# HGRN2 and latent-attention trunk on one core: block decays and 1/rms steps kept in PSUM, and two re-ordered entries

## The chip, the cores and the metric

The kernel runs on one core of a Trainium2 chip. The metric is the time of one execution in microseconds (us), as the device measures it. A kernel is run several times and the median counts.

## What is computed

Two layers over 1024 tokens of width 1024, all in float32. Cut to what matters:

```python
# layer 0
h = h + hgrn2_mixer(rmsnorm(h), ...)          # 8 heads of 128
h = h + square(relu(rmsnorm(h) @ w_up0)) @ w_dn0
# shared keys and values, then layer 1
ckr = rmsnorm(h) @ w_dkv                      # 256 latent + 64 rope columns
c_kv = rmsnorm(ckr[:, :256]); k_rope = rope(ckr[:, 256:])
c_q = rmsnorm(rmsnorm(h) @ w_dq)              # 256 columns
h = h + causal_attention(c_q @ w_uq, c_kv @ w_uk, c_kv @ w_uv, k_rope) @ w_o   # 16 heads
h = h + square(relu(rmsnorm(h) @ w_up1)) @ w_dn1
return rmsnorm(h)

def hgrn2_mixer(xn):                          # per head, chunks of 64 tokens
    q = silu(xn @ w_q); f = lb + (1 - lb) * sigmoid(xn @ w_f); k = 1 - f; v = xn @ w_i
    # inside a chunk: score(t, s) = sum_d q[t,d] * k[s,d] * prod(f[s+1..t, d]), s <= t
    # across chunks: state = prod(f) * state + (k * decays)^T v
```

## The kernel before

Every large product is made of three TensorE passes over operands split in a rounded part ("h") and a rest ("l"): wh·xh, wh·xl, wl·xh (`mm3`, line 99 for the projections). A weight that arrives by DMA is rounded on ACT (`load`, L135) and its rest is made on POOL (L138, a subtraction of two SBUF tiles of 128x1024). Work is written in program order with priorities, and a scheduler sets each engine's order from that; `tc.high_priority(offset)` moves a piece up, and `tc.issue_after(mark)` holds it behind a named matmul.

PSUM has eight banks of 128x512 float32: four of a tag `x` (HGRN) or `ps` (MLP) or two pairs of a tag `s` (attention), three of tag `mm`, and one, `nb`.

**HGRN (start to about 610 us).** 16 units, one for each head and half of the sequence. `project` makes the unit's f, k, q, values and gate by L99 matmuls; `core` makes the decayed scores. The products q·k with their decays are built by doubling block lengths h = 1, 2, 4, 8, 16, 32. At each length `grow` multiplies the k of the left half blocks (L342) and the q of the right half blocks (L344) by the block decay totals `tot`, and then multiplies neighbouring totals to those of the doubled blocks (L347), in SBUF tiles. For h of 4 and more the scores of a level are eight small matmuls (L366; two for each of four chunks) into a PSUM bank, of which columns 0 to 255 are used, and `put` (L323) copies them under a mask to ST. TensorE runs the level's L366 between the projections (L99) of the next unit.

**MLP.** Two-by-two block products by a seven-multiplication scheme; in `up_first` the products B11, B21, T1, B22, T2, T3, T4 of two halves e go to banks, and the combinations C00, C01, C11, C10 are summed on VectorE (DVE) (L729, L737, L739) and scaled by the token's 1/rms with the relu (L680). The 1/rms (`inverse`, L575 to L582) is a sum over partitions by a matmul, ACT's Ln and Exp, and one Newton step (`newton`, L110 to L112) over SBUF tiles. L818 are the matmuls of the product that follows (`down`), L802 adds their sums to the residual.

**Attention entry (1300 to 1410 us).** `cproj(w, i, u)` makes 128 columns i (0, 1: keys and values; 3, 4: queries; 2: rope) of half u: 24 L99 matmuls of 128x512 into one `mm` bank. After i = 1 it issues `inv_rms` (squares L481, sums L483, a matmul L489 behind the mark, then L491 to L493 and the Newton step), and L983 scales each bank by the result and frees it. The order is i = 0, 1, 3, 4, 2 for half 0 and then half 1, with `norm_kv` and `norm_q` (the second rmsnorms, again through L489, and L502, L92) between. L1107 are the score matmuls, L1147 transposes of probabilities, `fO` the outputs times w_o (L99 again).

## Time and profile before

| | |
|---|---|
| median of 3 runs | 2790.72 us (2789.53 to 2794.49) |
| profiled execution | 2790.73 us; its span 2788.9 us, so 1.8 us lie around the span |
| mean granted TensorE clock | 0.986 |
| TensorE busy | 2642.7 us (95%) |
| DVE, ACT, POOL busy | 1870.4, 1185.5, 1393.9 us |

"Idle before" is the time an engine sat still before an instruction, and the arrow names the engine, tile and line that released it. [...]

### The profile page before, as it was taken

How to read it: one execution, taken by the hardware profiler on the slowest of the kernel's cores; microseconds unless marked ns; L12 is line 12 of the kernel's file. 1: busy time of each engine (PE TensorE's matmuls, PEld its weight loads, DVE VectorE, ACT ScalarE, POOL GpSimd, SP SyncE). 2: the span in 40 equal slices, each digit the busy share in tenths (PEclk: the TensorE clock that was granted, in tenths of full speed). 3: DMA queues.
4: the chain of work that ended last, by engine and by line, in shares of the span. 5: the costliest groups of instructions: out<-in, count | busy, mean ns of one | idle time of the engine just before them, and what ended most of it. 6: DMA issues, size and time to landing. Idle time of an engine off the chain costs nothing.

```text
span 2788.9 us, 35224 instructions
## 1 busy us (share of the span) xinstructions
PE 2642.7 (95%) x13137; PEld 2182.1 (78%) x13137; DVE 1870.4 (67%) x2986; ACT 1185.5 (43%) x2262; POOL 1393.9 (50%) x865
## 2 busy tenths in 40 slices
PE   7999999999899999998799999999999899999997
PEld 6878877787688888877578888888877688888885
DVE  5566666658676666669776666676668755565667
ACT  4222223235334343446354444444445644444445
POOL 3222223456677777776221223122315677777776
PEclk9999999999999999999899999999999999999999
DMA  4111112242111111111111111111101211111111
GB/s 134 40 34 38 31 39 61 61 117 79 45 51 53 50 46 61 61 57 34 48 44 35 29 48 37 42 29 48 44 14 39 65 53 51 56 61 61 61 47 63
DMA packets 184632, 143.99 MB, mean 52 GB/s; under 512 B 12497, under 2 KB 156046, under 8 KB 184462
## 3 DMA queue, kind: packets, MB, share of 16 engines
q1 hardware_dynamic: 184462, 141.75, 16.8%
q8 instruction: 103, 1.69, 0.3%
q14 instruction: 67, 0.55, 0.1%
HBM read 133.33 MB, written 4.19 MB: 49 GB/s over the span
## 4 chain that ended last, share of the span: by engine, by line
PE 67%; DVE 13%; POOL 6%; issue 6%; ACT 5%; DMA 2%; SPq 0%; DVEq 0%; POOLq 0%; ACTq 0%
PE mm L99 21%; PE ps L818 8%; PE ps L669 7%; PE mm L669 7%; PE mm L818 6%; PE s L1107 5%; PE nb L1140 3%; POOL wl L534 3%; PE nb L818 2%; PE mm L1147 2%; PE x L366 2%; POOL wu L534 2%; DVE fr L534 1%; DMA dn<-mlp_w_down 1%; ACT P L1113 1%
## 5 line engine op out<-in xcount | busy, mean ns | idle before, releaser
L99 PE MATMUL mm<-xn,wh 128*128 128x512 f32 x1728 | 571.3, 405 | 10.9 <-DVE res L802 5.2
L534 POOL TENSOR_TENSOR wl<-dn,wh 128x512 fp32r<-128x512 f32 x224 | 367.5, 1661 | 137.7 <-ACT wh L621 121.6
L99 PEld LDWEIGHTS mm<-xn,wh 128*128 128x128 f32 x1728 | 322.9, 191 | 75.6 <-issue 8.9
L99 PE MATMUL mm<-xn,wl 128*128 128x512 f32 x864 | 347.8, 403 | 2.0 <-POOL wl L138 2.0
L138 POOL TENSOR_TENSOR wl<-wst,wh 128x1024 fp32r<-128x1024 f32 (+1 forms) x93 | 221.2, 2382 | 256.1 <-ACT wh L135 253.6
L534 POOL TENSOR_TENSOR wl<-wu,wh 128x512 fp32r<-128x512 f32 x160 | 232.2, 1462 | 62.3 <-ACT wh L621 60.4
L621 ACT CAST wh<-wu 128x512 fp32r<-128x512 f32 x216 | 130.6, 618 | 242.1 <-POOL wu L534 123.5
L792 ACT CAST hh<-fr 128x1024 fp32r<-128x1024 f32 x112 | 118.0, 1053 | 270.6 <-PE ps L818 132.4
L1116 POOL TENSOR_SCALAR P<-P,rc 128x128 f32<-128x128 f32 (+1 forms) x64 | 52.9, 826 | 347.9 <-DVE rc L1114 303.5
L534 POOL TENSOR_TENSOR wu<-wu,wu 128x512 f32<-128x512 f32 x120 | 175.1, 1459 | 92.8 <-DVE wl L534 42.1
L534 DVE TENSOR_TENSOR hl<-fr,hh 128x1024 fp32r<-128x1024 f32 x112 | 199.9, 1793 | 21.3 <-ACT hh L792 20.9
L534 POOL TENSOR_TENSOR dn<-dn 128x1024 f32<-128x1024 f32 x64 | 178.6, 2791 | 45.2 <-DMA dn<-mlp_w_down 41.4
L99 PEld LDWEIGHTS mm<-xn,wl 128*128 128x128 f32 x864 | 165.1, 191 | 33.9 <-POOL wl L138 2.4
L534 DVE TENSOR_TENSOR fr<-fr 128x1024 f32<-128x1024 f32 x68 | 131.7, 1937 | 50.3 <-ACT fr L675 48.7
L1113 ACT ACTIVATE P<-s,mx 128x384 f32<-128x384 f32 (+7 forms) x128 | 95.2, 743 | 138.6 <-DVE mx L1111 119.9
L621 ACT CAST wh<-dn 128x512 fp32r<-128x512 f32 x224 | 129.9, 615 | 25.2 <-PE ps L669 10.7
L1140 PE MATMUL nb<-h,xn 128*128 128x256 f32 (+1 forms) x640 | 134.2, 288 | 0.2
L1062 POOL TENSOR_TENSOR P<-P,sin 128x512 f32<-128x512 f32 x16 | 21.7, 1356 | 215.9 <-DMA P<-P 215.9
L669 PE MATMUL ps<-xn,wh 128*128 128x512 f32 x512 | 127.3, 390 | 2.3 <-DVE xn L534 1.5
L91 ACT CAST h<-mm 128x512 fp32r<-128x512 f32 (+1 forms) x160 | 82.8, 547 | 104.8 <-PE mm L1147 104.8
L669 PE MATMUL mm<-xn,wh 128*128 128x512 f32 x496 | 122.8, 389 | 0.0
L92 DVE TENSOR_TENSOR l<-mm,h 128x512 fp32r<-128x512 f32 (+1 forms) x160 | 97.0, 633 | 30.2 <-ACT h L91 29.9
(400 smaller groups left out, 6937.4 us busy)
## 6 DMA issues: line engine op xcount, KB each, us to landing
dn<-mlp_w_down SPq DMA_DIRECT2D x64, 512.0 KB, 3.9
wu<-mlp_w_up SPq DMA_DIRECT2D x122, 256.0 KB, 2.9
wst<-hgrn_w_o SPq DMA_DIRECT2D x16, 512.0 KB, 3.9
wst<-mla_w_o SPq DMA_DIRECT2D x16, 512.0 KB, 3.7
wst<-hgrn_w_q SPq DMA_DIRECT2D x10, 512.0 KB, 3.8
wst<-hgrn_w_i SPq DMA_DIRECT2D x10, 512.0 KB, 3.9
wst<-hgrn_w_g SPq DMA_DIRECT2D x10, 512.0 KB, 3.8
wst<-hgrn_w_f SPq DMA_DIRECT2D x9, 512.0 KB, 3.8
```

The source lines that it names most:

```text
L91: S.copy(out=out_h, in_=src)
L92: V.tensor_tensor(out=out_l, in0=src, in1=out_h.bitcast(F32), op=ALU.subtract)
L99: m = T.matmul(ps, l, r, start=i == 0, stop=i == n - 1)
L138: G.tensor_tensor(out=wl[:, cs], in0=st[:, cs], in1=wh[:, cs].bitcast(F32), op=ALU.subtract)
L534: return eng.tensor_tensor(out=out, in0=x, in1=y, op=op)
L621: S.copy(out=wh, in_=x)
L669: m = T.matmul(bank, l[:, k, :], r[:, k, :], start=start and n == 0, stop=n == 11, skip_group_check=not start)
L792: cast = S.copy(out=hh, in_=Bq)
L818: T.matmul(banks[i], l, r, start=start and k == 0 and n == 0, stop=k == 1 and n == 2, skip_group_check=not start)
L1107: T.matmul(ps[:, at + u * HALF:at + u * HALF + w_], l, r, start=e == 0, stop=e == len(terms) - 1)
L1113: S.activation(out=pt[:, :n], in_=sc, func=AF.Exp, bias=mx, accum_out=sm)
L1140: T.matmul(dst, l, r[:, cols_], start=j == 0 and e == 0, stop=j == 2 * g + 1 and e == 2)
```

## The change

1. **Decays.** `grow` gets a room in PSUM: the totals of h = 1, 2 are written to unused columns of the bank that held the sums of h = 1, those of h = 4 to 32 to columns 256 and up of the level's own score bank. The multiplications of k and q read the totals there; ACT copies each to SBUF, for the second operand of the next product.
2. **1/rms.** The variance and the Newton steps stand in the bank that the sum was made in.
3. **First MLP's `up_first`.** C11 += T3's bank and C01 += B22's come first (the one with a raised priority), then T4 of both halves, then the relus.
4. **Attention entry.** i = 0, 1 go to a pair of banks of tag `s`; the sums of squares are listed ahead; 1/rms comes after i = 3; the second norms move later; the first key and query products are held behind marks.
5. **Last outputs.** Three outputs of half 1 of the pair before go ahead of the last pair's outputs of half 0.

```diff
-            tot = f
+            tot = f, f
-            def grow(h, tot):
+            def grow(h, tot, room=None):
                 n = 512 // (2 * h)
-                t2 = tot.rearrange("p (b two) -> p b two", two=2)
+                t2, c2 = (t.rearrange("p (b two) -> p b two", two=2) for t in tot)
...
                 nt = sb(f"tot{h}", 2, (P, n))
-                V.tensor_tensor(out=nt, in0=t2[:, :, 0], in1=t2[:, :, 1], op=ALU.mult)
-                return nt
-            tot = grow(1, tot)
+                if room is None:
+                    V.tensor_tensor(out=nt, in0=t2[:, :, 0], in1=c2[:, :, 1], op=ALU.mult)
+                    return nt, nt
+                V.tensor_tensor(out=room, in0=t2[:, :, 0], in1=c2[:, :, 1], op=ALU.mult)
+                S.copy(out=nt, in_=room)
+                return room, nt
+            low = ps
+            tot = grow(1, tot, low[:, 256:512])
...
-            tot = grow(2, tot)
+            tot = grow(2, tot, low[:, 0:128])
...
-                tot = grow(h, tot)
+                tot = grow(h, tot, ps[:, 256:256 + 256 // h] if h < 64 else None)
+            tot = tot[1]
...
     def inv_rms(tmp, src, n, mark=None, acc=None):
+        acc = squared(tmp, src, n) if acc is None else acc
...
-        V.tensor_scalar(out=v, in0=ps, scalar1=1.0 / (n * P), scalar2=EPS, op0=ALU.mult, op1=ALU.add)
-        newton(y, v, t)
-        return y
+        V.tensor_scalar(out=ps, in0=ps, scalar1=1.0 / (n * P), scalar2=EPS, op0=ALU.mult, op1=ALU.add)
+        newton(y, ps, ps, None if n == KT else ps)
+        return y if n == KT else ps
...
-                V.tensor_scalar(out=acc, in0=ps, scalar1=1.0 / D, scalar2=EPS, op0=ALU.mult, op1=ALU.add)
-                newton(y, acc, t)
+                V.tensor_scalar(out=ps, in0=ps, scalar1=1.0 / D, scalar2=EPS, op0=ALU.mult, op1=ALU.add)
+                newton(y, ps, ps)
...
                 for e in two:
+                    with tc.high_priority(offset=40):
+                        V.tensor_tensor(out=C[e][1, 1], in0=C[e][1, 1], in1=x[e], op=ALU.add)
+                    V.tensor_tensor(out=C[e][0, 1], in0=C[e][0, 1], in1=z2[e], op=ALU.add)
+                each("T4", x, w, False)
+                for e in two:
+                    relu(0, C[e][1, 0], x[e])
+                for e in two:
                     relu(0, C[e][0, 0])
-                    V.tensor_tensor(out=C[e][0, 1], in0=C[e][0, 1], in1=z2[e], op=ALU.add)
+                    relu(1, C[e][1, 1])
                     relu(1, C[e][0, 1])
-                    V.tensor_tensor(out=C[e][1, 1], in0=C[e][1, 1], in1=x[e], op=ALU.add)
-                    relu(1, C[e][1, 1])
-                    product(x[e], w[e], "T4", False, True)
-                    relu(0, C[e][1, 0], x[e])
...
-            ps = bank()
+            if i == 0:
+                pairs[u] = bank2("s", 2, 1024)
+            ps = pairs[u][:, i * 512:(i + 1) * 512] if i < 2 else bank()
...
-                cmark.append(mm3(ps, [(wh[:, k, :], wl[:, k, :], xh[:, k, :], xl[:, k, :]) for k in range(KT)]))
-                if (i, u) in ((1, 0), (1, 1)):
-                    inv[u] = inv_rms(ntmp, lambda k: hT[u][:, k, :], KT, cmark[-1])
-                    for i, ps in held.pop(u, []) + [(i, ps)]:
+                terms = [(wh, xh, k) for k in range(KT)] + [(wl, xh, k) for k in range(KT)]
+                terms = terms[:4] + terms[8:12] + [(wh, xl, k) for k in range(4)] + terms[4:8] + terms[12:] + \
+                    [(wh, xl, k) for k in range(4, KT)]
...
+                if u not in inv:
+                    held.setdefault(u, []).append((i, ps))
+                if i == 3:
+                    inv[u] = inv_rms(ntmp, lambda k: hT[u][:, k, :], KT, cmark[-1], sums[u])
+                    for i, ps in held.pop(u):
                         scaled(i, u, ps)
...
+        sums = [squared(ntmp, lambda k: hT[0][:, k, :], KT)]
         for i in (0, 1, 3, 4, 2):
             cproj(wc[i], i, 0)
+        sums.append(squared(ntmp, lambda k: hT[1][:, k, :], KT))
...
+        cproj(wc[0], 0, 1)
+        with tc.high_priority(offset=150):
+            norm_kv(0, cmark[4])
+            norm_q(0, cmark[5])
...
-                todo = [t for t in todo if t[1] == 0] + [(p, 0, d) for d in range(KT)] + [t for t in todo if t[1]]
+                rest = [t for t in todo if t[1]]
+                todo = [t for t in todo if t[1] == 0] + rest[:3] + [(p, 0, d) for d in range(KT)] + rest[3:]
```

In the changed kernel the line numbers are a little higher: `grow` is L343, L345, L351 (L352 is the ACT copy), the level's matmuls L372, the entry's projections L994, the sums' matmul L500, the MLP's L740, L749, L748 stand for L729, L737, L739, and `down` is L832.

How the order moves, at three places. First DVE in HGRN, around the levels h = 4 to 16 of one unit (k_1082 and q_1111 before, k_1094 and q_1123 now); the names with f are the next unit's h = 1. Before:

```order
L323 COPY_PREDICATED ST_205<-masks,x_1533 112x16x16
L342 TENSOR_TENSOR k_1082<-k_1082,tot_286_1531 128x16x16
L344 TENSOR_TENSOR q_1111<-q_1111,tot_286_1531 128x16x16
L270 TENSOR_TENSOR prl_1756<-pr_1753,prh_1755 128x256
L342 TENSOR_TENSOR k_1378<-k_1378,f_1376 128x256
L344 TENSOR_TENSOR q_1407<-q_1407,f_1376 128x256
L323 COPY_PREDICATED ST_205<-masks,x_1543 96x8x32
L342 TENSOR_TENSOR k_1082<-k_1082,tot_288_1541 128x8x32
L344 TENSOR_TENSOR q_1111<-q_1111,tot_288_1541 128x8x32
```

Now:

```order
L323 COPY_PREDICATED ST_205<-masks,x_1533 124x64x4
L343 TENSOR_TENSOR k_1094<-k_1094,x_1507 128x64x4
L345 TENSOR_TENSOR q_1123<-q_1123,x_1507 128x64x4
L351 TENSOR_TENSOR x_1533<-x_1507,tot_282_1530 128x64
L270 TENSOR_TENSOR prl_1780<-pr_1777,prh_1779 128x256
L345 TENSOR_TENSOR q_1425<-q_1425,f_1394 128x256
L323 COPY_PREDICATED ST_205<-masks,x_1544 120x32x8
L343 TENSOR_TENSOR k_1094<-k_1094,x_1533 128x32x8
L345 TENSOR_TENSOR q_1123<-q_1123,x_1533 128x32x8
L351 TENSOR_TENSOR x_1544<-x_1533,tot_284_1541 128x32
```

The k and q products of a level now read a PSUM bank (x_...), and the product of totals (L351) stands inside the chain of levels; the levels lie later against the next unit's h = 1.

Second DVE in `up_first` of the first MLP, from the second half's Newton step to the sums that T4 waits for (ps_5723 and mm_5724, ps_5819 and mm_5820 are the banks of T3 and T4). Before:

```order
L112 SCALAR_TENSOR_TENSOR row<-hl_5638,row 128x512
L729 TENSOR_TENSOR fr<-fr,mm_5819 128x512
L737 TENSOR_TENSOR fr<-fr,ps_5866 128x512
L680 SCALAR_TENSOR_TENSOR fr<-fr,row 128x512 x2
L739 TENSOR_TENSOR fr<-fr,ps_5723 128x512
L737 TENSOR_TENSOR fr<-fr,nb_5867 128x512
L680 SCALAR_TENSOR_TENSOR fr<-fr,row 128x512 x2
L739 TENSOR_TENSOR fr<-fr,mm_5724 128x512
```

Now:

```order
L112 SCALAR_TENSOR_TENSOR row<-mm_5854,row 128x512
L749 TENSOR_TENSOR fr<-fr,ps_5962 128x512
L740 TENSOR_TENSOR fr<-fr,mm_5915 128x512
L691 SCALAR_TENSOR_TENSOR fr<-fr,row 128x512
L749 TENSOR_TENSOR fr<-fr,nb_5963 128x512
L748 TENSOR_TENSOR fr<-fr,ps_5819 128x512
L691 SCALAR_TENSOR_TENSOR fr<-fr,row 128x512 x3
L748 TENSOR_TENSOR fr<-fr,mm_5820 128x512
```

Of the four scaled relus (L680) that stood ahead of the sums for T4, one is left ahead of the first of them.

Third TensorE where the attention entry begins. Before:

```order
L818 MATMUL nb_10159<-hh_10358,wl_10367 128x512
L99 MATMUL mm_10577<-xn_10453,wh_10515 128x512
L99 MATMUL mm_10577<-xn_10454,wh_10515 128x512
L99 MATMUL mm_10577<-xn_10453,wl_10516 128x512
L99 MATMUL mm_10577<-xn_10453,wh_10515 128x512
```

Now:

```order
L832 MATMUL nb_10255<-hh_10454,wl_10463 128x512
L994 MATMUL s_10696<-xn_10549,wh_10611 128x512 x4
L994 MATMUL s_10696<-xn_10549,wl_10612 128x512 x4
L994 MATMUL s_10696<-xn_10550,wh_10611 128x512 x4
L994 MATMUL s_10696<-xn_10549,wh_10611 128x512 x4
L994 MATMUL s_10696<-xn_10549,wl_10612 128x512 x4
```

The first projection now goes to an `s` bank, the rests xl (xn_10550) and wl come after four matmuls of the rounded parts, and the sums' matmul L500 stands behind 72 of these matmuls, where L489 stood behind 49.

## Rows read from the trace of the kernel before

**Rows 1.** The page's part 1: TensorE's busy time, share of the span, instructions.
```profile
PE 2642.7 (95%) x13137; PEld 2182.1 (78%) x13137; DVE 1870.4 (67%) x2986; ACT 1185.5 (43%) x2262; POOL 1393.9 (50%) x865
```

**Rows 2.** Windows by stage: length, busy us of each engine, granted clock, DMA.
```profile
40.00:600.00 560.00, 536.22 (x2950) 440.50 (x2949) 350.92 (x904) 164.65 (x397) 160.22 (x86) 0.99 0.16 45
640.00:720.00 80.00, 70.54 (x295) 55.60 (x295) 66.81 (x65) 40.60 (x64) 45.73 (x24) 0.96 0.20 60
1300.00:1410.00 110.00, 82.77 (x335) 62.92 (x334) 84.82 (x114) 52.26 (x107) 33.15 (x21) 0.88 0.20 60
```

**Rows 3.** Waits of TensorE, 0 to 640 us: total, times, longest.
```profile
PE x L366 <- DVE q L344: 16.8, 12, 1.8
```

**Rows 4.** Timeline of all engines, 245.9 to 249.4 us: start, duration.
```profile
246.00 0.44 DVE L323 COPY_PREDICATED ST<-masks,x 96x256 f32<-96x256 uint8 x1
...
246.19 2.46 POOL L138 TENSOR_TENSOR wl<-wst,wh 128x1024 fp32r<-128x1024 f32 x1 [17.86 <-ACT wh L135]
...
246.34 2.59 DVE L342 TENSOR_TENSOR k<-k,tot 128x256 f32<-128x256 f32 x1
...
249.32 0.27 PE L366 MATMUL x<-q,k 128*64 128x64 f32 x1 [1.68 <-DVE q L344]
```

**Rows 5.** Single lines by form: ns min/median/max, first and last start.
```profile
L342 DVE TENSOR_TENSOR k<-k,tot x95: 403/417/2598, 79.2 to 588.7; 128x256 f32<-128x256 f32 x95
...
L402 ACT ACTIVATE on<-nb x64: 268/278/288, 94.3 to 595.1; 128x128 f32<-128x128 f32 x64
...
L135 ACT CAST wh<-wst x35: 1047/1052/1076, 63.8 to 504.6; 128x1024 fp32r<-128x1024 f32 x35
...
L92 DVE TENSOR_TENSOR xn<-res,xn x16: 678/683/2843, 1284.1 to 1312.0; 128x512 fp32r<-128x512 f32 x16
...
L802 DVE TENSOR_TENSOR res<-res,ps x112: 673/681/689, 715.4 to 1299.2; 128x512 f32<-128x512 f32 x112
```

**Rows 6.** Window in HGRN with one of those waits: the clock.
```profile
310.00:320.00 10.00, 8.30 (x46) 6.81 (x45) 8.26 (x20) 1.70 (x3) 2.46 (x1) 0.83 0.18 52
```

**Rows 7.** Timeline of TensorE, 245 to 251.5 us: a level's eight matmuls.
```profile
245.11 0.85 PE L366 MATMUL x<-q,k 128*96 128x64 f32 x8
```

**Rows 8.** Windows at the entry: TensorE's busy time and clock.
```profile
1305.00:1310.00 5.00, 4.25 (x10) 3.38 (x11) 4.74 (x7) 5.00 (x13) 2.11 (x1) 0.50 0.13 38
...
1380.00:1385.00 5.00, 5.00 (x22) 3.63 (x21) 3.41 (x4) 3.10 (x5) 3.90 (x3) 1.00 0.00 0
```

**Rows 9.** Timeline of DVE, 686 to 704 us, first MLP.
```profile
687.77 0.69 DVE L581 TENSOR_SCALAR hh<-ps 128x512 f32<-128x512 f32 x1 [3.79 <-ACT row L579]
...
690.08 2.26 DVE L111 TENSOR_TENSOR hl<-hl,row 128x512 f32<-128x512 f32 x1
...
700.96 0.68 DVE L739 TENSOR_TENSOR fr<-fr,ps 128x512 f32<-128x512 f32 x1
```

**Rows 10.** Timeline of TensorE, 695 to 711 us.
```profile
701.69 2.07 PE L669 MATMUL ps<-T4h,wh 128*128 128x512 f32 x4 [5.27 <-DVE fr L739]
...
706.98 1.18 PE L669 MATMUL mm<-T4h,wh 128*128 128x512 f32 x4
...
710.23 0.97 PE L818 MATMUL ps<-hh,wh 128*128 128x512 f32 x3 [0.24 <-ACT wh L621]
```

**Rows 11.** Timeline of TensorE, 1299 to 1330 and 1350 to 1380 us, attention entry.
```profile
1300.18 0.39 PE L818 MATMUL nb<-hh,wl 128*128 128x512 f32 x1
1305.75 1.22 PE L99 MATMUL mm<-xn,wh 128*128 128x512 f32 x2 [5.18 <-DVE res L802]
...
1364.92 2.07 PE L489 MATMUL nb<-acc,one 128*128 128x512 f32 x2 [10.52 <-DVE acc L483]
1371.58 1.19 PE L99 MATMUL mm<-xn,wh 128*128 128x512 f32 x2 [4.58 <-DVE P L983]
```

**Rows 12.** Timeline of DVE there: the sums of squares.
```profile
1312.75 8.05 DVE L483 TENSOR_TENSOR acc<-acc,s 128x512 f32<-128x512 f32 x7
```

**Rows 13.** Waits of TensorE, 2050 to 2180 us, end of the attention.
```profile
PE mm L99 <- POOL wl L138: 3.0, 2, 1.5
```

More of the change, by code (lines that the diff above doesn't have):

```diff
@@ L473, in build, with squared @@
         project_o(1, range(KT))
-    def inv_rms(tmp, src, n, mark=None):
+    def squared(tmp, src, n):
         acc = tmp("acc")
@@ L483, in inv_rms @@
                 V.tensor_tensor(out=acc, in0=acc, in1=sq, op=ALU.add)
+        return acc
+    def inv_rms(tmp, src, n, mark=None, acc=None):
+        acc = squared(tmp, src, n) if acc is None else acc
         ps = nbank()
@@ L489, in inv_rms @@
             T.matmul(ps, onef, acc, start=True, stop=True)
-        y, v, t = tmp("y"), tmp("v"), tmp("t")
+        y = tmp("y")
         S.activation(out=y, in_=ps, func=AF.Ln, scale=1.0 / (n * P), bias=eps)
         S.activation(out=y, in_=y, func=AF.Exp, scale=-0.5)
-        V.tensor_scalar(out=v, in0=ps, scalar1=1.0 / (n * P), scalar2=EPS, op0=ALU.mult, op1=ALU.add)
-        newton(y, v, t)
-        return y
+        V.tensor_scalar(out=ps, in0=ps, scalar1=1.0 / (n * P), scalar2=EPS, op0=ALU.mult, op1=ALU.add)
+        newton(y, ps, ps, None if n == KT else ps)
+        return y if n == KT else ps
     def fnorm(tmp, src, n, gain, outs, mark):
@@ L574, in inverse @@
             def inverse(u, mark, ps):
-                acc, y, t = accs[u], row[:, u], s_y[:, 1]
+                acc, y = accs[u], row[:, u]
                 with tc.issue_after(mark):
@@ L949, in build @@
         cmark, held = [], {}
+        pairs = {}
         def cproj(w, i, u):
@@ L970, in cproj @@
                 wh, wl = w
-                cmark.append(mm3(ps, [(wh[:, k, :], wl[:, k, :], xh[:, k, :], xl[:, k, :]) for k in range(KT)]))
-                if (i, u) in ((1, 0), (1, 1)):
-                    inv[u] = inv_rms(ntmp, lambda k: hT[u][:, k, :], KT, cmark[-1])
-                    for i, ps in held.pop(u, []) + [(i, ps)]:
+                terms = [(wh, xh, k) for k in range(KT)] + [(wl, xh, k) for k in range(KT)]
+                terms = terms[:4] + terms[8:12] + [(wh, xl, k) for k in range(4)] + terms[4:8] + terms[12:] + \
+                    [(wh, xl, k) for k in range(4, KT)]
+                for n, (l, r, k) in enumerate(terms):
+                    m = T.matmul(ps, l[:, k, :], r[:, k, :], start=n == 0, stop=n == len(terms) - 1)
+                cmark.append(m.ins)
+                if u not in inv:
[3 more added lines that the diff above has]
+                    for i, ps in held.pop(u):
                         scaled(i, u, ps)
-                elif u not in inv:
-                    held.setdefault(u, []).append((i, ps))
-                else:
+                elif u in inv:
                     scaled(i, u, ps)
@@ L1175, in build @@
             wc[i] = cload(i)
+        sums = [squared(ntmp, lambda k: hT[0][:, k, :], KT)]
         for i in (0, 1, 3, 4, 2):
             cproj(wc[i], i, 0)
+        sums.append(squared(ntmp, lambda k: hT[1][:, k, :], KT))
         ckv = xn_tile(0, "h").rearrange("p (s k t) -> p s k t", s=2, k=2)
         cq = xn_tile(0, "l").rearrange("p (s k t) -> p s k t", s=2, k=2)
-        with tc.high_priority(offset=100):
-            norm_kv(0, cmark[3])
+        cproj(wc[0], 0, 1)
+        with tc.high_priority(offset=150):
+            norm_kv(0, cmark[4])
+            norm_q(0, cmark[5])
         rope_k(0)
-        cproj(wc[0], 0, 1)
-        with tc.high_priority(offset=60):
-            norm_q(0, cmark[5])
         cproj(wc[1], 1, 1)
@@ L1188, in build @@
         cproj(wc[3], 3, 1)
-        fR(0, 0)
-        fK(0, 0)
         cproj(wc[4], 4, 1)
+        with tc.issue_after(cmark[-2]):
+            fR(0, 0)
+        with tc.issue_after(cmark[-1]):
+            fK(0, 0)
+        cproj(wc[2], 2, 1)
+        with tc.issue_after(cmark[-1]):
+            fQ(0, 0)
         with tc.high_priority(offset=60):
             norm_kv(1, cmark[-1])
-        fQ(0, 0)
-        cproj(wc[2], 2, 1)
         bigh, bigl = xn_tile(1, "h"), xn_tile(1, "l")
-        with tc.high_priority(offset=60):
-            norm_q(1, cmark[-1])
         rope_k(1)
         fV(0, 0)
+        norm_q(1, None)
         NG = 4 * HEADS_B
```

## The prediction

> **What bounds the kernel now.** I began with the busy times of the page: TensorE works 95% of the span [rows 1]. A change that leaves its matmuls as they are can therefore win only TensorE's idle time and the time that it runs at half clock. The windows by stage say how much there is where the change touches [rows 2]. Over 40 to 600 us TensorE is idle for 560 − 536.2 = 23.8 us, at a mean clock of 0.99. Over 640 to 720 us it is idle for 9.5 us, clock 0.96; over 1300 to 1410 us for 27.2 us, clock 0.88. After that I asked for TensorE's waits in each stage, to see which of them end where the change lies, and then for the timeline around the longest of each sort, to see why the releaser was late. The three stages together hold some 60 us of idle time. The missing clock times the length (5.6, 3.2 and 13.2 us) bounds what slow running cost in each; part of it passed idle and cost nothing.
>
> **A. Decays in PSUM.** The largest wait of HGRN is a level's matmuls behind the multiplication of q: 16.8 us in 12 waits [rows 3], 1.4 each. The timeline of one of them shows why [rows 4]: POOL's subtraction L138, 2.46 us long, starts at 246.19, and DVE's L342, which reads two SBUF tiles and starts 0.15 us later, takes 2.59 us and ends with it. L342 has a median of 0.417 us over 95 instructions, and 2.598 as its longest [rows 5]. So 2.2 us are lost on DVE each time, and 1.68 of them reach TensorE. With `tot` in PSUM, k and q read one SBUF tile. I expect them to pass beside POOL, since in the same stretch the DVE instructions with a PSUM operand keep their durations (L323, 0.44 us, as L138 starts [rows 4]). Of the DVE work that may still meet L138, the next unit's products with f read two SBUF tiles, and the order shows them a level earlier against POOL. I leave 0.3 us per wait, 3.6 in all, so 13.2 us go. A wait also drops the clock: 310 to 320 us has 1.70 us idle and a clock of 0.83 [rows 6], up to 1.7 us of lost speed; I count 2 us of the 3.4 that two such stretches would give.
>
> Against it: the totals' product (L351) is now inside the chain from one level to the next, and the levels begin 12 to 20 projection matmuls later. Per level the chain is 0.85 us for the eight matmuls [rows 7], 0.44 of `put` (L323 [rows 4]), and 0.42 each for k and q [rows 5], 2.1 us; TensorE has 7 or 8 projection matmuls of 0.227 us (22 in 5 us [rows 8]) and the eight themselves to fill it, about 2.4 to 2.6. The slack of 0.3 is easily spent by another DVE instruction that gets between, once per unit: 16 × 0.3 = 4.8 us. So A = −13.2 − 2 + 4.8, about **−10 us**; bounds −17 (all of the wait and half of the clock) and +2 (the wait finds another place and the slack is lost too, less what is left of the first).
>
> 96 copies of totals are new on ACT (6 for each of 16 units). The nearest row is a PSUM read of 128x128 on ACT, 0.278 us [rows 5]. A copy starts when L351 ends, as TensorE begins the level's eight matmuls; these and the `put` last 1.3 us [rows 4, 7], and k of the next level waits for the copy only after them. ACT is busy 164.65 us of 560 [rows 2]. I price it at nothing; its bound is 96 × 0.28 = 27 us if that cover fails.
>
> [...] The rows first: at 512 columns DVE takes 0.683 us with both inputs in SBUF (L92) and 0.681 us with one in PSUM (L802) [rows 5], so I price the PSUM operand at nothing. [...]
>
> **B. 1/rms in its bank.** It adds and removes nothing but SBUF tiles: the Newton steps get one SBUF input. In the first MLP one step of this kind took 2.26 us where the variance ahead of it took 0.69 [rows 9]; POOL was busy with subtractions then too. What it saves counts in D and C. The bank is held until the last step; at the first MLP T3 and T4 use other banks, at the entry `nb` is asked for again only by the next sum. No price.
>
> **D. First MLP's entry.** DVE goes from the first variance at 687.77 to the end of the first sum for T4 at 701.64, fifteen instructions of which the longest is 2.26 us [rows 9], and T4 starts at 701.69 after 5.27 us of idle [rows 10]. In the changed order 14 instructions lead to the same sum. At 0.66 us each (0.68 less overlap) that is 9.2 us: T4 starts near 697.2, 4.5 us sooner. Its first half took 706.98 − 701.69 = 5.29 us at half clock, where 12 matmuls at 0.227 need 2.7; after a wait under 1 us the clock should not fall, another 2.6. So TensorE would finish T4 about 7 us sooner, at 703; but the next product needs relu, rounding and rest of the first block, which now come after T4. T4's last bank is done near 702, the last sums near 701, and some 3 us of relu, rounding and rest follow the block that is ready first; L832 starts near 704 against 710.23 [rows 10]. D = **−6 us** (−3 if that chain takes 3 us longer, −7 if it is hidden). In the second MLP the order of this function is as it was, so nothing there.
>
> **C. Attention entry.** TensorE ends the MLP at 1300.4 and restarts at 1305.75, since its `mm` bank is freed by L802 late; then it runs at half clock, ten matmuls in 4.25 us [rows 8, 11], until about 1311. A bank of tag `s` is free at once, so the 72 matmuls ahead of the sums' matmul run from 1300.4 to 1316.7; half of their weights' rests come just in time. L500 then waits for the sums of squares, since ACT's and DVE's orders up to them are unchanged: seven L483 from 1312.75 to 1320.80 [rows 12]. So there is a new wait of 4.1 us, but 72 matmuls lie ahead of it and not 49; a gain of 23 × 0.227 = 5.2 us. If those 4.1 us drop the clock as the 5.18 did, 2.4 us go back; I take half of that: −4.0.
>
> The next hole is larger: 10.52 us for the second sums, two matmuls at half clock (2.07 us, half of it lost), and 4.58 us for a bank that waits for 1/rms [rows 11], then 4.7 us at half clock, half of them lost: 18.5 us. The changed kernel sums half 1's squares while TensorE still works on half 0, and 48 matmuls of half 1 have banks before any 1/rms of it. So all of it goes. But the second norms (three matmuls L500 with a DVE chain of 8 to 10 instructions ahead of each) stand now among half 1's projections; they seem in step to within 0 to 3 us, and I put back 4.5 in all. C = −4.0 − 18.5 + 4.5 = **−18 us**, bounds −25 (no new waits, clock up) and −11 (the first gain nil, the chains 3 us late each).
>
> **E. Last pair's outputs.** TensorE waits twice, 3.0 us in all, for the rest of the first w_o tile on POOL [rows 13]. Three outputs of the pair before, 18 matmuls or 4.1 us, now come ahead. E = **−2.8 us** (−1 to −3).
>
> **The sum.** −10 − 6 − 18 − 2.8 = −37. The profiled execution took 2790.73 us and the median is 2790.72, so the sum holds for both: 2790.7 − 37 = **2754 us**.
>
> **The rivals.**
> *The collision only moves.* L138 is still 2.4 us long; the products with f, and the rests of rounded sums (L270), still read two SBUF tiles, and one of them may now be the one that POOL meets. For it: which instruction was hit was a matter of a tenth of a microsecond [rows 4]. Against: k and q of five of six levels can no longer be hit, and what still can is not all on the chain. A = 0: 2790.7 − 27 = 2764.
> *A PSUM operand costs DVE more.* L323, with a PSUM operand of 256 columns, took 0.44 us [rows 4] where L342 from SBUF has 0.417 [rows 5]: 0.023 us more for k and q at five levels of 16 units, 160 × 0.023 = 3.7 us if all of it is exposed, so 2758. Against it stands the pair at 512 columns. [...]
> *The entry is bound by DVE.* In 1300 to 1410 DVE is busy 84.8 of 110 us [rows 2], more than TensorE; if the new order only shifts the same chain, C gives 8 and not 18: 2764 again.
> *The copies on ACT are exposed, and it gets slower.* k of the next level waits for ACT, which works in order: a copy behind L135 (1.05 us [rows 5]) or a sigmoid that itself waits for TensorE holds DVE, the level, and then TensorE. A copy costs 0.28 us, and if it stands on average 0.3 us behind another, 96 × 0.58 = 56 us are added and the 13 us of the collision are still won: 2790.7 − 27 + 43 = 2807. It decides from (27 + 13)/96 = 0.42 us of exposure per copy; below that it only eats the gain. Against it stand the 1.3 us of cover.
> *It does little.* If DVE's long instructions have another cause than two SBUF inputs beside POOL, A and B give nothing, and the gains at the entries shrink with them; with the copies partly exposed too, 2785 to 2795.
>
> **How the numbers follow.** The forecast case has 0.60, the moved collision 0.17, the dearer PSUM operand 0.03, the entry bound by DVE 0.12, little or nothing 0.04, exposed copies 0.04, of which one part in four still ends within 0.2%. A measurement of this kernel can tell about 0.2% (5.6 us) from no change. Faster 0.92, same 0.05, slower 0.03. The range: all low bounds together, 17 + 7 + 25 + 3 = 52, are unlikely at once; I go to 2738. Above, both middle rivals at once give 2774.
>
> **What would show it.** TensorE's wait for q at a level should fall from 16.8 to under 5 us, and DVE's longest k from 2.6 to under 0.6. T4's wait should be under 1.5 us, with the clock at 1.00 after it. The entry should show no idle at its first projection, one wait of 3 to 5 us for the first sums, and no 10 us hole. At the end, no wait for POOL at the outputs. ACT's 96 copies should release no wait of DVE that TensorE inherits. The forecast is wrong if HGRN's length (16 units of about 32 us) does not fall, or if the entry stays longer than 97 us.

## The result and the profile after

The changed kernel takes 2761.24 us (median of 4 runs, 2760.56 to 2763.45) where the kernel before took 2790.12 us beside it (4 runs, 2786.4 to 2794.49): a ratio of 0.9897, 95% interval 0.9882 to 0.9913. That is 29 us faster, where 37 were forecast; the time lies inside the range of 2738 to 2774 us. The profiled span went from 2788.9 to 2758.6 us.

To see which part gave what, take the same matmul in both traces and compare when it starts. Single lines by form, with first and last start after the durations, of the kernel before (the MLP's products L669 and L818, the output products on L99):

```profile
L669 PE MATMUL mm<-xn,wh x496: 388/389/481, 660.0 to 2708.6; 128*128 128x512 f32 x166
...
L818 PE MATMUL ps<-hh,wh x224: 387/389/501, 710.2 to 1293.2; 128*128 128x512 f32 x112
...
L99 PE MATMUL mm<-oh,wh x256: 387/389/501, 1463.9 to 2132.6; 128*128 128x512 f32 x128
```

The same three of the changed kernel:

```profile
L680 PE MATMUL mm<-xn,wh x496: 387/389/476, 647.4 to 2678.2; 128*128 128x512 f32 x166
...
L832 PE MATMUL ps<-hh,wh x224: 389/389/628, 690.7 to 1271.0; 128*128 128x512 f32 x112
...
L99 PE MATMUL mm<-oh,wh x256: 387/389/471, 1436.3 to 2102.1; 128*128 128x512 f32 x128
```

Five of these times cut the span into stages (the last start of the first line lies in the second MLP and is not used). The last column gives the same stage in the profiles of all kernels that were run, with the part and without it, since a single profile is not exact to more than 2 or 3 us (the third row's stage, with the same products in every kernel, took 579.4 to 585.0).

| stage | before | after | difference | forecast | all profiles without the part, with it |
|---|---|---|---|---|---|
| start to the MLP's first product (A) | 660.0 | 647.4 | −12.6 | −10 | 658.2 to 661.2; 645.7 to 649.8 |
| to its second product (D, B) | 50.2 | 43.3 | −6.9 | −6 | 49.8 to 50.2; 43.1 to 44.1 |
| to the last of these | 583.0 | 580.3 | −2.7 | 0 | 579.4 to 585.0 with and without any part |
| to the first output product (C) | 170.7 | 165.3 | −5.4 | −18 | 170.7 to 174.0; 162.5 to 165.4 |
| to the last output product (E) | 668.7 | 665.8 | −2.9 | −2.8 | 668.7 to 670.3; 664.5 to 666.6 |
| to the end | 656.3 | 656.5 | +0.2 | 0 | |

(In the last column, the values with A and with C are those of kernels that have the part as the change makes it; the experiments' variants of it are told below.) D and E came as forecast, and A gave somewhat more. C gave a third to a half of its term. It fell short by 10 to 12.6 us, more than the 7 to 8 us by which the result missed the forecast: A's 2.6 us, D's 0.9 and the 2.7 us in the row that no part touches hid most of the rest.

**HGRN.** TensorE's waits from 0 to 640 us (total, times, longest); before, the first of them was 16.8 us behind q [rows 3]:

```profile
PE x L274 <- DVE prl L270: 4.7, 10, 0.5
PE x L372 <- DVE x L351: 3.2, 4, 1.1
...
PE x L372 <- DVE q L345: 0.2, 1, 0.2
```

Lines by form, ns min/median/max, of the changed kernel, where k and q read a PSUM bank (x) or, at h = 1, the tile f:

```profile
L343 DVE TENSOR_TENSOR k<-k,x x96: 398/410/475, 79.0 to 580.1; 128x256 f32<-128x256 f32 x96
L343 DVE TENSOR_TENSOR k<-k,f x15: 415/422/2480, 87.7 to 543.5; 128x256 f32<-128x256 f32 x15
...
L345 DVE TENSOR_TENSOR q<-q,x x96: 405/411/474, 79.3 to 580.4; 128x256 f32<-128x256 f32 x96
...
L270 DVE TENSOR_TENSOR prl<-pr,prh x46: 407/680/2605, 78.4 to 565.4; 128x512 fp32r<-128x512 f32 x31, 128x256 fp32r<-128x256 f32 x15
```

None of the 192 multiplications with a PSUM operand takes over 0.475 us; before, the longest had 2.598 [rows 5]. A count over the timelines tells whether the operand or the new order did this. Before, 11 of the 190 multiplications by `tot` start while an L138 runs, and each of them takes 1.41 to 2.60 us. Now 28 of 192 start while one runs, and none of those takes over 0.42 us. The timeline shows one such pair, k and q (POOL, then DVE, 242 to 246 us):

```profile
242.47 2.40 POOL L138 TENSOR_TENSOR wl<-wst,wh 128x1024 fp32r<-128x1024 f32 x1 [18.45 <-ACT wh L135]
```

```profile
242.07 0.42 DVE L345 TENSOR_TENSOR q<-q,f 128x256 f32<-128x256 f32 x1
...
243.40 0.41 DVE L343 TENSOR_TENSOR k<-k,x 128x256 f32<-128x256 f32 x1
243.73 0.41 DVE L345 TENSOR_TENSOR q<-q,x 128x256 f32<-128x256 f32 x1
...
244.16 0.99 DVE L286 TENSOR_SCALAR f<-sg,oml,lb 128x512 f32<-128x512 f32 x1
```

What POOL's subtraction still holds are instructions that read only SBUF: those left with two SBUF tiles (k with f up to 2.480 us, prl up to 2.605), and also L286, which reads one tile (0.99 us above, where its median before was 0.535). DVE at 402 us, 0.45 us after an L138 has started:

```profile
402.43 2.22 DVE L286 TENSOR_SCALAR f<-sg,oml,lb 128x512 f32<-128x512 f32 x1 [0.34 <-ACT sg L284]
```

TensorE pays for some of these. Three of the four waits behind L351 (0.96, 0.96 and 1.11 us) follow an L286 of 2.22 us or an L270 of 2.60, and one of 1.58 us at 546.42 follows the k with f of 2.48. The waits behind L270 itself grew from 1.6 to 4.7 us in all, none over 0.5.

The clock of the stage rose as well (0.99 to 1.00), and so did its work: 545.7 us of TensorE in the window that had 536.2 [rows 2]. Two windows of the changed kernel, the second moved by the 22 us that the entry begins sooner:

```profile
40.00:600.00 560.00, 545.71 (x3014) 445.84 (x3013) 340.12 (x914) 189.56 (x505) 164.68 (x90) 1.00 0.18 50
1278.00:1388.00 110.00, 89.97 (x364) 68.91 (x363) 81.76 (x124) 55.12 (x115) 30.37 (x22) 0.88 0.21 60
```

In the entry's window TensorE is idle for 20.0 us where it was 27.2, and its clock is 0.88 as it was: the waits have moved more than they shrank.

**First MLP.** T4 had waited 5.27 us and then run at half clock [rows 10]: the granted clock was 0.50 from 701 to 707 us. Timeline of TensorE in the changed kernel, where it is 1.00 from 684.24 to 689.5:

```profile
684.24 1.20 PE L680 MATMUL ps<-T4h,wh 128*128 128x512 f32 x4 [0.44 <-DVE fr L748]
...
687.11 1.07 PE L680 MATMUL mm<-T4h,wh 128*128 128x512 f32 x4
...
690.71 1.21 PE L832 MATMUL ps<-hh,wh 128*128 128x512 f32 x4 [0.72 <-ACT wh L632]
```

DVE there, from the first variance to the first sum that T4 waits for:

```profile
675.14 0.70 DVE L592 TENSOR_SCALAR ps<-ps 128x512 f32<-128x512 f32 x1 [3.80 <-ACT row L590]
...
683.51 0.67 DVE L748 TENSOR_TENSOR fr<-fr,ps 128x512 f32<-128x512 f32 x1
```

**Attention entry.** TensorE's waits, 1270 to 1430 us:

```profile
PE mm L99 <- DVE P L1007: 7.9, 1, 7.9
PE nb L500 <- DVE acc L489: 4.7, 2, 4.3
PE s L1131 <- ACT P L1137: 3.2, 1, 3.2
PE mm L99 <- DVE oh L983: 2.8, 1, 2.8
```

The 10.52 us are gone, and so is the idle start; but a hole of 7.9 us has taken their place. The reader can follow it back over four engines. TensorE, DVE, POOL and SP's DMA queue, each a timeline of the changed kernel:

```profile
1278.20 1.07 PE L994 MATMUL s<-xn,wh 128*128 128x512 f32 x4
...
1298.95 2.08 PE L500 MATMUL nb<-acc,one 128*128 128x512 f32 x2 [4.27 <-DVE acc L489]
1300.04 2.70 PE L994 MATMUL mm<-xn,wh 128*128 128x512 f32 x4
...
1346.51 1.19 PE L99 MATMUL mm<-xn,wh 128*128 128x512 f32 x2 [7.92 <-DVE P L1007]
```

```profile
1332.50 0.70 DVE L504 TENSOR_SCALAR nb<-nb 128x512 f32<-128x512 f32 x1 [1.65 <-ACT y L502]
1338.69 1.52 DVE L1025 TENSOR_TENSOR oh<-oh,ol 64x512 f32<-64x512 f32 x1 [5.49 <-POOL ol L1024]
1340.13 0.68 DVE L110 SCALAR_TENSOR_TENSOR nb<-nb,y 128x512 f32<-128x512 f32 x1
1340.89 2.06 DVE L92 TENSOR_TENSOR kr_l<-oh,kr_h 64x512 fp32r<-64x512 f32 x1
```

```profile
1334.32 1.28 POOL L1023 TENSOR_TENSOR oh<-oh,cos 64x512 f32<-64x512 f32 x1 [2.51 <-DMA cos<-cosd]
1335.57 1.84 POOL L138 TENSOR_TENSOR wl<-wst,wh 128x768 fp32r<-128x768 f32 x1
1337.37 1.28 POOL L1024 TENSOR_TENSOR ol<-ol,sin 64x512 f32<-64x512 f32 x1
```

```profile
1329.51 0.47 SPq L1039 DMA_DIRECT2D wst<-kv_w_uv  x1
1330.08 0.41 SPq L930 DMA_DIRECT2D cos<-cosd  x1
```

The first key product needs a bank that L1007 frees with the 1/rms of half 1. That Newton step (L110) stands on DVE behind the rope's addition of half 0 (L1025), which waits 5.49 us for POOL's second product; POOL had waited for the cosine table, which SP issued behind the first pair's weights, and put a weight's rest (L138) between the two products. A second instruction of the rope, the rest of the rotated keys (L92, 2.06 us), stands inside the Newton step. What TensorE needed next was ready to be computed at 1333.2.

### The profile page after: what moved, and what is told of

It reads as the page before. It is cut to its first block, busy times and chain, and to the rows that moved or that the text cites. A ratio compares the mean times of both kernels' runs of the same rounds, so it can differ in the third digit from the quotient of the medians.

```text
span 2758.6 us, 35383 instructions
## 1 busy us (share of the span) xinstructions
PE 2643.0 (96%) x13137; PEld 2183.8 (79%) x13137; DVE 1852.5 (67%) x2986; ACT 1204.5 (44%) x2358; POOL 1389.6 (50%) x865
## 4 chain that ended last, share of the span: by engine, by line
PE 38%; DVE 7%; ACT 3%; issue 2%; DMA 0%; POOL 0%; SPq 0%; DVEq 0%; ACTq 0%; POOLq 0%
PE mm L99 8%; PE s L1131 6%; PE mm L680 5%; PE ps L832 5%; PE ps L680 4%; PE nb L1164 4%; PE mm L832 3%; PE mm L1171 2%; PE nb L832 1%; DVE res L818 1%; DVE fr L545 1%; ACT P L1137 1%; DVE hl L545 1%; DVE P L1085 1%; DVE xn L1095 1%
## 5 line engine op out<-in xcount | busy, mean ns | idle before, releaser
L99 PE MATMUL mm<-xn,wh 128*128 128x512 f32 x1600 | 526.0, 404 | 12.3 <-DVE P L1007 7.9
L138 POOL TENSOR_TENSOR wl<-wst,wh 128x1024 fp32r<-128x1024 f32 (+1 forms) x93 | 220.4, 2373 | 261.0 <-ACT wh L135 225.7
L99 PEld LDWEIGHTS mm<-xn,wh 128*128 128x128 f32 x1600 | 295.1, 190 | 68.5 <-issue 10.3
L99 PE MATMUL mm<-xn,wl 128*128 128x512 f32 x800 | 321.0, 401 | 2.0 <-POOL wl L138 2.0
L99 PEld LDWEIGHTS mm<-xn,wl 128*128 128x128 f32 x800 | 151.5, 189 | 32.3 <-POOL wl L138 2.4
L680 PE MATMUL ps<-xn,wh 128*128 128x512 f32 x512 | 127.3, 390 | 2.3 <-DVE xn L545 1.5
L680 PE MATMUL mm<-xn,wh 128*128 128x512 f32 x496 | 122.8, 389 | 0.0
L92 DVE TENSOR_TENSOR l<-mm,h 128x512 fp32r<-128x512 f32 (+1 forms) x160 | 96.9, 633 | 30.1 <-ACT h L91 29.8
```

The costliest lines, as they stand in the source:

```text
L92: V.tensor_tensor(out=out_l, in0=src, in1=out_h.bitcast(F32), op=ALU.subtract)
L99: m = T.matmul(ps, l, r, start=i == 0, stop=i == n - 1)
L138: G.tensor_tensor(out=wl[:, cs], in0=st[:, cs], in1=wh[:, cs].bitcast(F32), op=ALU.subtract)
L680: m = T.matmul(bank, l[:, k, :], r[:, k, :], start=start and n == 0, stop=n == 11, skip_group_check=not start)
```

## The experiments

The first three ask whether the parts add up: each is the kernel before with one part of the diff as it stands.

**Decays alone** (`grow` and its calls).
```diff
-            def grow(h, tot):
+            def grow(h, tot, room=None):
...
```


> The kernel before with the decays in PSUM alone (part A). In the changed kernel the first matmul of the first MLP starts at 647.4 us where it started at 660.0, so theory 1 (the parts add up, and all of this comes from A): 12.6 us faster than before, 2777 to 2779 us, TensorE's wait for q at a level under 1 us. Rival (A gains only together with the other parts, or the traced shift is chance): under 6 us faster.

Measured: 2782.75 us against 2791.6, ratio 0.9965 (0.9951 to 0.9979), some 10 us faster with an interval of 6 to 14; the MLP begins at 649.3 us. That is less than the 12.6 expected, and above the rival's 6; in the profile the stage is 10.7 us shorter. A stands by itself, and the wait for q is 0.2 us in total.

**First MLP alone** (sums ahead, 1/rms in its bank).
```diff
+                    with tc.high_priority(offset=40):
+                        V.tensor_tensor(out=C[e][1, 1], in0=C[e][1, 1], in1=x[e], op=ALU.add)
...
+                newton(y, ps, ps)
```


> The kernel before with the first MLP's order of sums and its 1/rms in the bank alone (parts D and B there). From the two traces the stretch from the MLP's first matmul to the end of the MLP is 9.6 us shorter, 6.9 of it at the entry and 2.7 in the loop behind. Theory 1: 9 to 10 us faster. Rival (the 2.7 us of the loop come from other parts, by where the MLP's start falls): 7 us faster, the loop as long as before.

Measured: 2782.31 us, ratio 0.9967 (0.9954 to 0.9979), some 9 us faster. In the profile the entry takes 44.1 us and the loop behind it 581.6, which lies in the range that every kernel shows there. So 6 us are the entry's, and the rest is within the interval: the 2.7 us of the two traces are not to be put down to the change.

**Attention entry alone** (`cproj`, `inv_rms` and the list of projections and norms).
```diff
+            if i == 0:
+                pairs[u] = bank2("s", 2, 1024)
+            ps = pairs[u][:, i * 512:(i + 1) * 512] if i < 2 else bank()
...
+                if i == 3:
+                    inv[u] = inv_rms(ntmp, lambda k: hT[u][:, k, :], KT, cmark[-1], sums[u])
```


> The kernel before with the attention entry alone (part C and the 1/rms in the bank there). Theory 1: 5 to 6 us faster, as the traces show, and not the 18 forecast: a new wait of about 8 us at the first key product behind DVE L1007's counterpart, since the rope's addition stands ahead of half 1's Newton step on DVE, and one of about 4 us for the first sums. Rival (the hole is made by other parts that shift the DMAs): 12 us or more faster, no wait over 5 us there.

Measured: 2781.51 us, ratio 0.9963 (0.9951 to 0.9976), some 10 us faster with an interval of 7 to 14, between the two expectations. The trace decides for the first: the entry takes 165.4 us, 5.3 less than before, with waits of 8.9 and 4.2 us at the two places (L997 and L482 there are L1007 and L489):

```profile
PE mm L99 <- DVE P L997: 8.9, 1, 8.9
PE nb L493 <- DVE acc L482: 4.7, 2, 4.2
```

The holes belong to C itself. The other 4 us by which this profile is shorter lie in stages that C does not touch, 2.9 of them in the MLP's loop.

**The rope behind the scalings.** The changed kernel, one line moved:
```diff
-        rope_k(0)
         cproj(wc[1], 1, 1)
         load_pair(0)
         cproj(wc[3], 3, 1)
         cproj(wc[4], 4, 1)
+        rope_k(0)
```


> The changed kernel with one line moved: the rope of half 0 is listed behind the fourth projection of half 1, so that DVE's addition of the rotated keys (L1025) stands behind the four scalings by 1/rms of half 1 and not ahead of its Newton step. Theory 1 (DVE waits 5.5 us in order for POOL's rope product, and TensorE's 7.9 us and its half clock are that wait handed on): 7 to 9 us faster than the changed kernel, 2752 to 2754 us, that wait gone. Rival (TensorE would wait there anyway, for the second norms or the scores' keys): 0 to 3 us faster, another wait of 5 us or more within the next 20 us.

Measured: 2753.58 us, ratio to before 0.9863 (0.985 to 0.9877), 7.7 us under the changed kernel's 2761.24, and the two intervals lie apart. The entry falls from 165.3 to 154.2 us, the wait of 7.9 us is gone, and none over 4.2 us takes its place. DVE's timeline:

```profile
1333.49 0.70 DVE L504 TENSOR_SCALAR nb<-nb 128x512 f32<-128x512 f32 x1 [1.66 <-ACT y L502]
1334.30 0.70 DVE L110 SCALAR_TENSOR_TENSOR nb<-nb,y 128x512 f32<-128x512 f32 x1
...
1338.97 0.93 DVE L1025 TENSOR_TENSOR oh<-oh,ol 64x512 f32<-64x512 f32 x1
```

The step follows the variance at once, and the rope's addition waits for nothing, since its inputs are ready by then. The cause is shown: the rope's place in DVE's order, ahead of the Newton step and inside it.

**Reading the copy in SBUF.** The changed kernel, but the totals are read from ACT's copy:
```diff
                 S.copy(out=nt, in_=room)
-                return room, nt
+                return nt, nt
```


> The changed kernel, except that k, q and the next total read ACT's copy in SBUF and not the totals in PSUM; the order of DVE's instructions is the same. Theory 1 (an instruction with two SBUF inputs is held by POOL's subtraction of two SBUF tiles, and reading PSUM ends that): some L343 or L345 of the levels take 2.4 to 2.6 us again where the changed kernel has 0.475 at most, TensorE waits for q 8 us or more, and 6 to 14 us are lost against the changed kernel. Rival 1 (the new order alone keeps the levels clear of POOL): all stay under 0.6 us, 0 to 3 us lost, from the copy's place in the chain. Rival 2 (the copy is now in the chain and costs more than the collision): 10 us or more lost with no instruction over 0.6 us.

Measured: 2777.34 us, ratio 0.9955 (0.9943 to 0.9967), 16 us slower than the changed kernel; the MLP begins at 666.4 us, later than in the kernel before. (DVE's order is nearly but not wholly the same: some neighbours change places.) Waits of TensorE, 0 to 640 us, and two lines by form:

```profile
PE x L372 <- DVE x L351: 16.6, 11, 1.9
...
PE x L372 <- DVE q L345: 2.0, 7, 0.5
```

```profile
L345 DVE TENSOR_TENSOR q<-q,tot x96: 408/415/2576, 79.3 to 599.4; 128x256 f32<-128x256 f32 x96
...
L351 DVE TENSOR_TENSOR x<-tot x80: 162/191/2368, 80.2 to 597.7; 128x128 f32<-128x128 f32 x16, 128x64 f32<-128x64 f32 x16, 128x32 f32<-128x32 f32 x16, 128x16 f32<-128x16 f32 x16
```

With the second input in SBUF the long instructions are back in about the new order, and 16.6 us of waits with them. The waits are not for q, as expected, but for L351, which DVE runs right behind q. Eight of the 11 follow a multiplication or total of the levels that took 1.96 us or more, two the next unit's q with f (2.6 us), one an L286 of 2.22. The loss is a little over the 14 us expected. Waits for the copy do not explain it: DVE's come to 1.7 us in this trace. Where the operand lies makes A; the order alone, as near as this kernel has it, gains nothing.

**Two copies.** The copy is made twice, to the same tile, in one kernel; in another a second one goes to a tile that nobody reads.
```diff
                 S.copy(out=nt, in_=room)
+                S.copy(out=nt, in_=room)
```


> The changed kernel with each of the 96 copies of the totals on ACT made twice; a copy has a median of 0.194 us in the profile, so 96 of them are 18.6 us of ACT more. Theory 1 (the copies lie beside the level's matmuls and its masked copy): within 0 to 3 us of the changed kernel, no wait of DVE for ACT that TensorE inherits. Rival (part of A's expected gain is lost since k of the next level waits for the copy): 5 to 19 us slower than the changed kernel.


```diff
                 S.copy(out=nt, in_=room)
+                S.copy(out=sb(f'twin{h}', 2, (P, n)), in_=nt)
```


> The changed kernel with a second copy of each total on ACT, from the first copy to another SBUF tile that nobody reads: 96 copies more, right behind the first ones, while the orders of DVE and TensorE in HGRN stay those of the changed kernel (in the run with two copies to the same tile they did not). Theory 1 (the 6 us lost there came from the re-ordering, and copies as such are hidden): within 2.5 us of the changed kernel, HGRN's end between 645 and 650 us. Rival (96 copies cost ACT's place on the chain of levels): 5 us or more slower, HGRN's end at 653 us or later.

Measured: the first 2768.27 us, ratio 0.992 (0.9908 to 0.9933), 7 us slower than the changed kernel, and the MLP begins at 655.4; the second 2761.07 us, ratio 0.9903 (0.9888 to 0.9918), no different from it, MLP at 646.2. In the first the scheduler also put DVE's and TensorE's instructions in another order, in the second it did not. So ACT's time for 96 copies more costs nothing with the order held. That the first copy holds nobody up is read from the traces: of DVE's waits from 60 to 640 us, none is for a copy, in the changed kernel and in both of these. This speaks for the new order as the cause of the first kernel's loss, but no run separates the two.

**Sums of squares first.** The kernel with the rope moved, and half 0's squares raised:
```diff
-        sums = [squared(ntmp, lambda k: hT[0][:, k, :], KT)]
+        with tc.high_priority(offset=100):
+            sums = [squared(ntmp, lambda k: hT[0][:, k, :], KT)]
```


> The kernel with the rope moved (e4_rope_behind), and half 0's sums of squares raised in priority, so that on DVE they stand among the rests of half 1's rounded inputs and not behind them, and on ACT ahead of half 1's roundings. Theory 1 (TensorE's 4.2 us for the first sums and the half clock behind it, about 2.5 us more, are that place in the order): 4 to 7 us faster than with the rope moved, 2747 to 2750 us, that wait under 1 us and the clock at 1.00 behind it. Rival (the weights of the later projections, which ACT now scales 3 us later, end the wait instead): 0 to 2 us faster, a wait for POOL's rest or ACT's rounding of a weight there.

Measured: 2753.74 us, ratio 0.987 (0.9856 to 0.9885): the same as with the rope moved. The rival was right. The entry takes 155.6 us, the wait for the sums is 0.4 us, and in its place TensorE waits for a weight's rest, whose scaling and rounding on ACT had been put off by the squares:

```profile
1296.96 2.07 PE L994 MATMUL mm<-xn,wl 128*128 128x512 f32 x4 [4.69 <-POOL wl L138]
```

**Half 1's inputs later.** Also on the kernel with the rope moved; what makes room on ACT and DVE is now work that TensorE needs last:
```diff
-            for k in range(KT):
-                split(xh[:, k, :], xl[:, k, :], hT[u][:, k, :])
+            with tc.high_priority(offset=-120 * u):
+                for k in range(KT):
+                    split(xh[:, k, :], xl[:, k, :], hT[u][:, k, :])
```


> The kernel with the rope moved (e4_rope_behind), and the rounding and rests of half 1's inputs lowered in priority, so that on ACT the last squares stand ahead of them and the weight of the third projection is scaled as early as in the changed kernel. Theory 1 (the wait for the first sums can go without a wait for a weight in its place): the entry, 154.2 us from the MLP's last product to the first output in the run with the rope moved, becomes 148 to 151 us, and the kernel is 3 to 6 us faster than that one, 2748 to 2751 us. Rival (half 1's inputs become late and end the next wait): 153 us or more, with a wait for a rounded input or its rest.

Measured: 2749.03 us, ratio 0.9849 (0.9836 to 0.9863), the lowest median of all: 12 us under the changed kernel. Its interval overlaps that of the kernel with the rope moved (0.985 to 0.9877), so the gain of 4.5 us over that one is likely but not shown. The trace agrees with the expectation: the entry takes 150.4 us, and the wait for the first sums, 4.2 us in the kernel with the rope moved, is 1.3. Waits of TensorE there:

```profile
PE s L1132 <- ACT P L1138: 2.5, 1, 2.5
PE s L1132 <- DVE Ql L92: 2.4, 1, 2.4
PE nb L500 <- DVE acc L489: 1.8, 2, 1.3
```

**The MLP's two edits apart.** The order of the sums without the bank, and the bank without the order, on the kernel before:
```diff
+                each("T4", x, w, False)
```


> The kernel before with the first MLP's order of sums alone, the Newton steps still over SBUF tiles (part D without B). With both, from the MLP's first matmul to the first of its second product there are 44 us where there were 50. Theory 1 (the place of DVE's sums and the steps held beside POOL each make half of it): 46 to 48 us there, T4's wait 2 to 4 us with the clock falling. Rival (the order is all of it): 44 us.


```diff
-                newton(y, acc, t)
+                newton(y, ps, ps)
```


> The kernel before with the first MLP's Newton steps in the sum's bank alone (part B there without D's order). Order alone left the stretch from the MLP's first to its second product at 49.5 us, both together made it 44.1. Theory 1 (the two gains hide each other: T4 comes after the steps and after the sums, and each alone leaves the other as the end of the wait): 47 to 50 us there, T4's wait 3 to 5 us, 0 to 3 us faster than before. Rival (the steps held beside POOL were all of it): 44 to 45 us, 6 us faster.

Measured: the order alone 2787.23 us, ratio 0.999 (0.9981 to 1.0), not to be told from the kernel before, the entry 49.5 us and T4 4.6 us late; the bank alone 2785.03 us, ratio 0.9978 (0.9969 to 0.9987), the entry 45.8 us and T4 1.8 us late. The waits, order first:

```profile
PE ps L669 <- DVE fr L737: 4.6, 1, 4.6
```

```profile
PE ps L669 <- DVE fr L739: 1.8, 1, 1.8
```

Both together had 44.1. So of some 6 us the steps in PSUM give 4.4, the order alone 0.7 (hardly more than the spread of kernels without either, 49.8 to 50.2), and on top of the steps 1.7. The first of my theories (each makes half) is wrong, and so is the second (each alone hides the other): the steps were most of it.

**Outputs as before.** The changed kernel without part E:
```diff
-                todo = [t for t in todo if t[1] == 0] + rest[:3] + [(p, 0, d) for d in range(KT)] + rest[3:]
+                todo = [t for t in todo if t[1] == 0] + [(p, 0, d) for d in range(KT)] + [t for t in todo if t[1]]
```


> The changed kernel with the order of the last pair's outputs as before (without part E). Theory 1 (E takes away the two waits for POOL's rest of the output weights): the stretch from the first to the last output is 668 to 670 us and not 665.8, those two waits of 1.5 us are back, 2 to 4 us slower than the changed kernel. Rival (something else shortened that stretch): 665 to 667 us.

Measured: 2764.95 us, ratio 0.9906 (0.9891 to 0.992), whose interval overlaps the changed kernel's; the trace has 668.8 us from first to last output, and the two waits are back:

```profile
PE mm L99 <- POOL wl L138: 3.0, 2, 1.6
```

## Why the prediction was right, and where it was off

**A, −10 forecast, −12.6 in the trace.** The mechanism was the one named: DVE's two-SBUF instructions held by POOL's subtraction (before, 1.41 to 2.60 us for the 11 that started beside one, 0.417 the median of k [rows 5]). The experiment with the SBUF operand brings the waits back. The rival that the new order alone kept the levels clear is out: 28 multiplications start beside an L138, and none is held (0.42 us at most). Left at the levels are 3.4 us (3.6 foreseen). The expectation that the collision would meet other instructions instead came true as well (k with f up to 2.48 us, so the sign of 0.6 us for the longest k holds for the levels alone; L270 up to 2.605; and L286 up to 2.22, which the prediction did not name). Some 4.6 us of it reached TensorE. In all, TensorE's idle time from 40 to 600 us fell by 9.5 us (23.8 to 14.3), so other waits took back about 4 of the 13.4 won behind q, near the 4.8 put against the change. The 3 us or so that are left of the 12.6 would be the clock (0.99 to 1.00 over the stage), of which 2 were counted.

One step of the working is wrong without harm: the prediction lets k of the next level wait for ACT's copy, but as the diff has it, k and q read the bank, and only the next product of totals reads the copy.

The rival that a PSUM operand costs DVE more is out too: k reads PSUM in 0.410 us (median) where it took 0.417 from SBUF [rows 5].

**D, −6, measured −6.9.** T4 waits 0.44 us (under 1 was said) and runs at full clock (1.00; its first four matmuls take 1.20 us, where they took 2.07 [rows 10]). The step by which the first sum would be ready 9.2 us after the variance holds: from 675.14 to 684.18 us it is 9.0. The prediction did not say which of the two edits does what; the steps in the bank do most of it.

**E, −2.8, measured −2.9.** Both waits are gone.

**C, −18, measured −5.4 (about −8 between the means of all profiles).** The first half was right: TensorE starts at 1278.2 with no idle time, then waits 4.27 us for the first sums (4.1 said) and runs at half clock behind them (0.50 from 1300 to 1305 us; the next four matmuls take 2.70 us, and four at 1278.20 took 1.07); I had taken half of that loss. The step that failed is the next: "So all of it goes", with 4.5 us put back for norms that "seem in step to within 0 to 3 us". I had counted the matmuls that can run before half 1's 1/rms, and the DVE instructions ahead of each norm, but not what those instructions wait for. The rope was listed by the change behind the second norms, with its table's DMA behind the first pair's weights on SP and its products among weights on POOL; on DVE its addition stood one place ahead of the Newton step, which did not pass it: ready at 1333.2, the step began at 1340.13. That put 7.9 us and some half clock (0.57 over 1345 to 1350 us) where the 18.5 had been. With the rope moved the entry is 16.5 us shorter than before (170.7 to 154.2), near the 18 of the term. The prediction's own sign said so too: the entry, 110 us long before, stayed longer than 97, at 102 to 105. That the total still came within 8 us of the forecast is in part luck, since A and the MLP's loop gave 5.3 us more than was forecast for them, half of that by the spread between profiles.

Of the rivals, two had the time nearest to the result (2764). "The collision only moves" is refuted as the whole of A by the 12.6 us. "The entry is bound by DVE" had even the size of C (8 us) but not the reason: DVE stood idle for 5.49 us in the hole. The exposed copies are refuted by the run with twin copies and by DVE's waits, and "it does little" by A, C, and D with B, each of which makes the kernel some 9 to 10 us faster alone.

## What to carry to other kernels

Where DVE's multiplications of two SBUF tiles start while POOL works on two SBUF tiles, put one operand of them in PSUM, if a bank has columns to spare; here the 28 that started beside a 2.4 us subtraction took 0.42 us at most, where such ones had taken up to 2.60. When an order is changed, look on each engine at the instruction just ahead of the one that TensorE waits for, and ask what that one waits for, back through POOL and the DMA queue: the cost of a step is what it blocks and not what it takes (the rope's addition took 1.52 us, and the hole behind it was 7.9). And an earlier sum is worth nothing if it pushes back a weight that is needed as soon (2753.74 us against 2753.58); take the place from work that is needed last (here the wait shrank from 4.2 to 1.3 us, and the gain in time is likely but within the intervals).

## What was not expected of the hardware

The time from the first MLP's second product to its end (the same products in every kernel) varied between 579.4 and 585.0 us from profile to profile, without order by the parts. So a stage's difference of 2 or 3 us between two single traces shows nothing, and several profiles of each sort were needed to read D and E.

The operand's place shows in the durations alone: with the totals' product, the k and the q at the same columns, 0.19 or 0.41 us is the median whether they read PSUM or SBUF, and the maximum tells them apart (0.475 at most against 2.3 to 2.6).
